# Interleaving two arrays on one core: the second x tile comes in as four DMAs with 8 KiB rows

## The chip, the cores and the metric

The kernel runs on one core of one Trainium2 chip. The metric is the device time of one execution in microseconds (us). Before the change the median of three runs is 314.51 us (314.41 to 314.53).

## The reference

Two float32 arrays x and y of shape 32 x 256 x 1024 are woven into one of shape 32 x 256 x 2048: x goes to the even places of the last axis and y to the odd ones.

```python
def reference(x, y):
    batch, seq, dim = x.shape
    result = np.zeros((batch, seq, dim * 2), dtype=np.float32)
    result[..., 0::2] = x
    result[..., 1::2] = y
    return result
```

No arithmetic is done. 33.55 MB of x, 33.55 MB of y and 67.11 MB of output are moved.

## The kernel before, in words

Since the last axis of the output is just twice as long, the arrays are taken as flat. They are cut into n = 8 tiles. A tile of x or y is 128 partitions by W = 8192 floats, so each partition holds one contiguous row of 32 KiB and the tile 4 MiB. The 8 MiB of output that belong to a tile are made in two halves h = 0, 1, each from H = 4096 columns of the x tile and of the y tile, and each stored as a tile of 128 x 8192.

There are two buffers each for x (`xt`), y (`yt`) and the output (`ot`). Tile k uses `xt[k % 2]` and `yt[k % 2]`; half h uses `ot[h]`. The program is written out by hand for three engines, which meet only through semaphores:

- SP issues all loads (queue q1 of the profile). The first x tile comes as two DMAs of half the columns (L37 and L38, rows of 16 KiB), then y 0, x 1, y 1 without any wait (L48 and L45). From tile 2 on, x (L45) waits until DVE has read the second half of the x tile two before, that is until `woven` has reached 4(k-2)+3, and y (L48) until it has reached 4(k-2)+4.
- DVE (VectorE) weaves. For each tile and half it copies the x half into the even places of `ot[h]` (L60) and the y half into the odd places (L63). Each copy counts `woven` up by one. Before L60 it waits for the x tile (`xsem`; `hsem` for the second half of the first tile) and for the store that last read `ot[h]` (`osem`); before the L63 of a first half it waits for the y tile (`ysem`).
- ACT (ScalarE) only issues stores (L68, queue q10): one of 4 MiB for each half, 16 in all, each when `woven` says that both copies of the half are done.

The loads of SP and the stores of ACT run on the same 16 DMA engines. A DMA counts its semaphore up by 16, one for each engine, as its parts land. At the end ACT waits for the last store of `ot[0]` and clears the range of semaphores, and SP waits for the last store of `ot[1]`. The wrapper moves SP's first two DMAs ahead of the opening barrier of the program.

Of the kernel before, what the change touches and what calls it, by code (L numbers as in the profile page):

```python
# [3 lines left out]


def _interleave(nc, x, y, out):
    P = 128
    W = 8192
    H = W // 2  # L10

    total = 1
    for s in x.shape:
        total *= s
    n = total // (P * W)
    assert n * P * W == total

    def rows(ap, names, k):
        flat = ap.rearrange("b s d -> (b s d)")
        return flat[k * names : (k + 1) * names].rearrange("(p w) -> p w", p=P)  # L20

    fp32 = mybir.dt.float32
    xt = [nc.alloc_sbuf_tensor(f"xt{b}", [P, W], fp32).ap() for b in (0, 1)]
    yt = [nc.alloc_sbuf_tensor(f"yt{b}", [P, W], fp32).ap() for b in (0, 1)]
    ot = [nc.alloc_sbuf_tensor(f"ot{b}", [P, W], fp32).ap() for b in (0, 1)]

    xsem = [nc.alloc_semaphore(f"xsem{b}") for b in (0, 1)]
    hsem = nc.alloc_semaphore("hsem")
    ysem = [nc.alloc_semaphore(f"ysem{b}") for b in (0, 1)]
    woven = nc.alloc_semaphore("woven")  # L30
    osem = [nc.alloc_semaphore(f"osem{b}") for b in (0, 1)]

    xs = [rows(x, P * W, k) for k in range(n)]
    ys = [rows(y, P * W, k) for k in range(n)]
    os_ = [rows(out, 2 * P * W, k) for k in range(n)]

    nc.sync.dma_start(out=xt[0][:, :H], in_=xs[0][:, :H]).then_inc(xsem[0], 16)  # L37
    nc.sync.dma_start(out=xt[0][:, H:], in_=xs[0][:, H:]).then_inc(hsem, 16)  # L38

    for k in range(n):  # L40
        b = k % 2
        if k >= 2:
            nc.sync.wait_ge(woven, 4 * (k - 2) + 3)
        if k:
            nc.sync.dma_start(out=xt[b], in_=xs[k]).then_inc(xsem[b], 16)  # L45
        if k >= 2:
            nc.sync.wait_ge(woven, 4 * (k - 2) + 4)
        nc.sync.dma_start(out=yt[b], in_=ys[k]).then_inc(ysem[b], 16)  # L48

    for k in range(n):  # L50
        b = k % 2
        for h in (0, 1):
            c = slice(h * H, (h + 1) * H)
            if h == 0:
                nc.vector.wait_ge(xsem[b], 16 * (k // 2 + 1))
            elif k == 0:
                nc.vector.wait_ge(hsem, 16)
            if k:
                nc.vector.wait_ge(osem[h], 16 * k)
            nc.vector.tensor_copy(out=ot[h][:, 0::2], in_=xt[b][:, c]).then_inc(woven, 1)  # L60
            if h == 0:
                nc.vector.wait_ge(ysem[b], 16 * (k // 2 + 1))
            nc.vector.tensor_copy(out=ot[h][:, 1::2], in_=yt[b][:, c]).then_inc(woven, 1)  # L63

    for k in range(n):
        for h in (0, 1):
            nc.scalar.wait_ge(woven, 4 * k + 2 * h + 2)
            nc.scalar.dma_start(  # L68
                out=os_[k][:, h * W : (h + 1) * W], in_=ot[h]
            ).then_inc(osem[h], 16)  # L70

    nc.scalar.wait_ge(osem[0], 16 * n)
    used = sorted(s.num for s in [*xsem, hsem, *ysem, woven, osem[0]])
    assert used == list(range(used[0], used[-1] + 1)), used
    nc.scalar.sem_clear(range(used[0], used[-1] + 1))
    nc.sync.nop(nofuse=True).wait_op(osem[1], 16 * n, "sem-ge").then_inc(
        osem[1], -16 * n
    )


def kernel(tc, x, y, out):
    nc = tc.nc
    tc.close()
    tc.compile()

    _interleave(nc, x, y, out)

    blocks = nc.main_func.blocks
    for engine in (mybir.EngineType.SP, mybir.EngineType.SP):
        opening = blocks[0].instructions  # L90
        at, moved = next(
            (b, i)
            for b in blocks[1:]
            for i in b.instructions
            if i.engine == engine and i.opcode == "DMACopy"
        )
        assert not (moved.sync_info and moved.sync_info.on_wait)
        body = at.instructions
        body.remove(moved)
        gate = next(  # L100
            n
            for n, i in enumerate(opening)
            if i.engine == engine and i.opcode == "Drain"
        )
        opening.insert(gate, moved)
        at.instructions = body
        blocks[0].instructions = opening


# [1 line left out]
_INS = ['x', 'y']  # L111
_OUTS = [((32, 256, 2048), 'float32')]


# [23 lines left out]
```

## Time and profile before

| | |
|---|---|
| median of 3 runs | 314.51 us (314.41 to 314.53) |
| the profiled execution: its time, its span | 314.29 us, 313.0 us |
| DMA queue q1 (loads): packets, share of 16 engines | 2448, 50.1% |
| DMA queue q10 (stores): packets, share of 16 engines | 2304, 49.7% |
| mean rate over the span, read and written together | 429 GB/s |
| DVE busy | 72.6 us (23%), 32 copies of 2.3 us |
| L60 idle before, waiting for stores | 171.5 us of 178.8 |
| L63 idle before, waiting for y | 46.7 us |

The span is the time between the first and the last recorded event of the profiled execution; the device time is a little more. The page gives the busy time of each engine, the DMA activity in 40 equal slices, the DMA queues, and the chain of work that ended last, followed back from the end. The timeline and the chain list start and length in microseconds from the span's start, and in brackets the idle time before an instruction with what ended it. An idle time of DVE costs nothing by itself, if the DMA engines are busy meanwhile.

### The profile page before, as it was taken

To read this page: it belongs to the slowest core of one execution; us is meant where nothing else is said; L and a number is where in the kernel's file an instruction comes from. 1 tells how busy PE (TensorE), PEld (TensorE's weight loads), DVE (VectorE), ACT (ScalarE), POOL (GpSimd) and SP (SyncE) were. 2 spreads that over 40 slices of the span, in tenths; PEclk is the share of its full clock that TensorE was granted. 3 is DMA by queue.
4 is the path that set the end of the run, shared out by engine and by line. 5 is a ranking of instruction groups with operands and counts; after the bars stand their busy time and mean duration, and the time that the engine had idled before them with its cause. 6 is when DMAs were issued, how large, how long until landed. Compare 5 with 4: busy or idle time off the path is not lost.

```text
span 313.0 us, 113 instructions
## 1 busy us (share of the span) xinstructions
DVE 72.6 (23%) x32; POOL 0.2 (0%) x4
## 2 busy tenths in 40 slices
DVE  0226002231022410325003150031501305013510
POOL 0000000000000000000000000000000000000000
DMA  8999999999999999999999999999999999999998
GB/s 341 463 410 394 469 402 448 423 436 436 419 452 406 465 402 469 402 469 402 469 402 448 423 436 436 419 452 406 465 402 469 402 469 402 465 406 444 427 431 373
DMA packets 4752, 134.22 MB, mean 429 GB/s; under 512 B 528, under 2 KB 528, under 8 KB 528
## 3 DMA queue, kind: packets, MB, share of 16 engines
q1 hardware_dynamic: 2448, 67.11, 50.1%
q10 hardware_dynamic: 2304, 67.11, 49.7%
HBM read 67.11 MB, written 67.11 MB: 429 GB/s over the span
## 4 chain that ended last, share of the span: by engine, by line
DMA 82%; DVE 12%; issue 0%
DMA out_dram<-ot 76%; DVE ot L63 6%; DMA yt<-in_y_dram 6%; DVE ot L60 6%
## 5 line engine op out<-in xcount | busy, mean ns | idle before, releaser
L60 DVE COPY ot<-xt 128x4096 f32<-128x4096 f32 x16 | 36.7, 2295 | 178.8 <-DMA out_dram<-ot 171.5
L63 DVE COPY ot<-yt 128x4096 f32<-128x4096 f32 x16 | 36.7, 2292 | 46.7 <-DMA yt<-in_y_dram 46.7
L122 POOL MEMSET const-bfloat16-1.0<- 128x1 bf16 x1 | 0.1, 101 | 0.0
L122 POOL MEMSET const-uint8-127<- 128x1 uint8 x1 | 0.1, 101 | 0.0
L122 POOL MEMSET const-float32-0.0<- 128x1 f32 x1 | 0.1, 98 | 0.2 <-issue 0.2
L122 POOL MEMSET const-float32-1.0<- 128x1 f32 x1 | 0.1, 98 | 0.0
## 6 DMA issues: line engine op xcount, KB each, us to landing
out_dram<-ot ACTq DMA_DIRECT2D x16, 4096.0 KB, 29.1
yt<-in_y_dram SPq DMA_DIRECT2D x8, 4096.0 KB, 60.8
xt<-in_x_dram SPq DMA_DIRECT2D x7, 4096.0 KB, 43.7
xt<-in_x_dram SPq DMA_DIRECT2D x2, 2048.0 KB, 9.5
```

Of the source, the lines that this page charges most:

```text
L60: nc.vector.tensor_copy(out=ot[h][:, 0::2], in_=xt[b][:, c]).then_inc(woven, 1)
L63: nc.vector.tensor_copy(out=ot[h][:, 1::2], in_=yt[b][:, c]).then_inc(woven, 1)
L122: nc = _bacc.Bacc("TRN2", target_bir_lowering=False, num_devices=1)
```

## The change

The load of the second x tile (k = 1) is cut into four DMAs of a quarter of the columns each. A row of such a DMA is 2048 floats, 8 KiB. The four are issued one after the other at the place of the one before, between y 0 and y 1. The first three count a new semaphore `qsem` (48 when all have landed), the fourth counts `xsem[1]` as the whole load did. DVE waits for `qsem` as well before the first L60 of tile 1, and the new semaphore is cleared with the others at the end. All other loads and all stores are as before, and the order of the instructions on DVE and ACT is the same.

```diff
+    qsem = nc.alloc_semaphore("qsem")
...
+    quarters = [slice(q * W // 4, (q + 1) * W // 4) for q in range(4)]
...
-        if k:
+        if k == 1:
+            for c in quarters[:3]:
+                nc.sync.dma_start(out=xt[b][:, c], in_=xs[k][:, c]).then_inc(qsem, 16)
+            c = quarters[3]
+            nc.sync.dma_start(out=xt[b][:, c], in_=xs[k][:, c]).then_inc(xsem[b], 16)
+        elif k:
             nc.sync.dma_start(out=xt[b], in_=xs[k]).then_inc(xsem[b], 16)
...
                 nc.vector.wait_ge(xsem[b], 16 * (k // 2 + 1))
+                if k == 1:
+                    nc.vector.wait_ge(qsem, 48)
...
-    used = sorted(s.num for s in [*xsem, hsem, *ysem, woven, osem[0]])
+    used = sorted(s.num for s in [*xsem, hsem, qsem, *ysem, woven, osem[0]])
```

## The prediction

> **What bounds the kernel now.** I read the page first, then the chain that ended last, then the timeline of the first tiles, then five-microsecond windows around the place of the change, and last the trace's records of single DMA packets and landings, which no view prints and which I give as numbers.
>
> The page, its head, the strip of DMA busy tenths and the queues:
>
> ```profile
> span 313.0 us, 113 instructions
> ...
> DMA  8999999999999999999999999999999999999998
> ...
> DMA packets 4752, 134.22 MB, mean 429 GB/s; under 512 B 528, under 2 KB 528, under 8 KB 528
> ...
> q1 hardware_dynamic: 2448, 67.11, 50.1%
> q10 hardware_dynamic: 2304, 67.11, 49.7%
> ```
>
> The two queues (q1 carries SP's loads, q10 ACT's stores) fill 50.1 + 49.7 = 99.8% of what 16 engines can give in the span. DVE is busy 23%. The kernel is a DMA stream without holes; only holes in it, or dearer packets, can move the time. The 528 small packets are semaphore writes (33 DMAs x 16 engines). The other 4224 are whole rows: 31 whole DMAs and 2 halves at 128 rows each make 33 x 128 = 4224. So one packet is one row, 32 KiB long, or 16 KiB in the first x tile, and each of the 16 engines takes 8 rows of every DMA.
>
> The chain (start, length, what) says what sets the order inside the stream:
>
> ```profile
> 1.90 19.98 DMA yt<-in_y_dram
> ...
> 21.90 2.30 DVE ot L63
> 24.20 2.20 DVE ot L60
> 26.40 2.21 DVE ot L63
> ...
> 28.63 38.64 DMA out_dram<-ot
> ```
>
> After that a store of 34 us and two DVE copies repeat to the end. A store takes 34 us although its 4 MiB alone would take 9.7, because two stores and the loads share the engines. The timeline shows the first tiles:
>
> ```profile
> 21.90 2.30 DVE L63 COPY ot<-yt 128x4096 f32<-128x4096 f32 x1 [12.30 <-DMA yt<-in_y_dram]
> ...
> 24.23 72.37 ACTq L68 DMA_DIRECT2D out_dram<-ot  x5
> ...
> 26.43 0.33 SPq L45 DMA_DIRECT2D xt<-in_x_dram  x1
> ...
> 48.01 2.30 DVE L60 COPY ot<-xt 128x4096 f32<-128x4096 f32 x1 [19.41 <-DMA out_dram<-ot]
> 55.22 2.29 DVE L63 COPY ot<-yt 128x4096 f32<-128x4096 f32 x1 [4.91 <-DMA yt<-in_y_dram]
> 67.29 2.30 DVE L60 COPY ot<-xt 128x4096 f32<-128x4096 f32 x1 [9.78 <-DMA out_dram<-ot]
> ```
>
> The first y tile lands at 21.9, the first store is issued at 24.23, and the second x tile runs on q1 from about 21.5, so most of it shares the engines with the first stores. In the packet records a 32 KiB row takes 1.213 us on one engine whatever the mix, a 16 KiB row 0.611, and once both queues have work they take strict turns, one row each. The windows (stretch, DVE and POOL busy, clock, DMA share by packet starts, GB/s) show the one hole after the start:
>
> ```profile
> 20.00:25.00 5.00, 3.10 (x2) 0.00 (x0) 1.00 1.11 478
> 25.00:30.00 5.00, 3.60 (x2) 0.00 (x0) 1.00 0.91 328
> 30.00:35.00 5.00, 0.00 (x0) 0.00 (x0) 1.00 0.97 419
> ```
>
> In 25 to 30 the rate falls to 328 GB/s. The packet records say why: the two load rows ahead of the first store row take 1.2 to 1.6 and 1.7 to 1.9 us instead of 1.213. Added up this is 0.74 us on each engine. It comes as the store queue starts from empty beside running loads (store issued 24.23, first store row 29.06, six rows of x done by then). No later stretch has it: from 40 to 290 us all rows together exceed 1.213 by under 0.01 us per engine. The other start of an empty queue, SP's at 1.0 us, stretched its first rows by 0.65 us.
>
> **The change, part by part.** *Issues.* SP issues four DMAs instead of one behind the first y: three more at 0.33 to 0.44 us (the rows of its issues), 1.0 to 1.3 us. Queued behind is the second y's issue, at 2.76, now near 4. Its first row cannot run before the second x is through, after 35 us, so this costs nothing; the cover is over 30 us. *The wait on qsem.* It goes into the set that DVE's L60 for the second tile waits for already; three quarters have landed before the fourth on the same queue, apart from fractions of a microsecond. Behind it on DVE stands L63, which waits for y until later. Zero.
>
> *Dearer rows.* The trace has no 8 KiB row of a load. By the landings, two 2 MiB halves take 2 x 4.88 = 9.76 us (7.28 to 12.16 is the second), a whole 4 MiB 9.67 (the last store, 303.27 to 312.94) or 9.72 (first y, 12.16 to 21.88). One cut costs 0.04 to 0.09, three cuts 0.12 to 0.27. I take 0.2 us, the three additional semaphore packets of 9 ns included. This is on the path, since the stream has no slack.
>
> *Turns.* If a turn stays one row, the second x gives 0.3 us away per turn and receives 1.2 us of store. By the time of the first store row (26 to 29 us) 15 to 23 of its 32 rows per engine are through. The first store then needs 8 x (1.21 + 0.31) = 12 us and lands near 39 to 42 instead of 47.9. The second ends at about 26.8 + 16 x 1.21 + 17 x 0.31 = 51.5 when the join is early, and near 58.5 when it is late (x exhausted after some ten turns, six store rows shared with y rows). Both lie before the second y, which ends when everything so far is through: 21.9 + four times 9.67 + 0.2 + 0.74 = 61.5 us. DVE can't make a new store without that y, so **the store queue runs empty**, which it never did between 29 and the end. The loads fill the gap (third x and y were issued at 26.4 and 28.6), so no bandwidth is lost by that alone.
>
> But from here the state is the one of 21.9 us again, a tile later: y lands, no store is queued, x and y of the next tile stand on SP's queue, and DVE goes L63, L60, L63. The store queue starts from empty a second time, at about 63.9 (61.5 + 2.35). Bounds of that start: 0 (no later stretch pays it) to 0.74, or a little more. I take 0.74, because this is the same transition with the same row sizes, and SP's start at 1.0 us paid a similar 0.65. What the first start costs with short rows beside it is not shown; between -0.74 and +0.74, I take no change, as the stretching began 1.8 us after the store's issue and so seems to follow it rather than the loads' rows.
>
> *Afterwards.* As the second tile's start repeats the first tile's, the distance between loads and stores repeats too: before, y lands at 55.2 and the second store of the tile before at 67.3, and at the end 287.5 against 293.6; this holds five store rows, enough to hide the last L63 and the next store's way to the engines (issue at 289.89, first row 293.25). Cost zero if the distance is the same.
>
> Sum: 0.20 + 0.74 = **+0.94 us**. The profiled execution has span 313.0 and time 314.29; it becomes 313.9 and 315.23. The median before is 0.22 above that execution, so the forecast is 314.51 + 0.94 = **315.45**.
>
> **The rivals.** (1) *The restart is free*, not slower: the stretch at 26 us belonged to the first store of the program, not to the queue being empty. For it: all of 40 to 290 us is clean. Against: the queue was never empty there. It decides if the second start costs under 0.43 us (0.63 less the 0.20). Time 314.51 + 0.20 = 314.7. If the first start also shrinks with short rows, 0.74 is given back: 313.97.
>
> (2) *The queue does not run empty*, the change doesn't do what it says: turns go by bytes, or by several short rows. Then landings stay as before and only 0.20 is left: 314.7. For: no mix of unequal rows is in the trace, since the 16 KiB rows ran alone. Against: with 32 KiB rows a turn was exactly one. The Trainium skill, "DMA: Bandwidth & Descriptors", section "Queues, rings and completion order", has engines change queues at packets, which hold some 9 to 17 descriptors as a rule. The one-row turns of this trace disagree for long rows; for 8 KiB rows no run here shows it yet.
>
> (3) *The distance comes back a row shorter*, five x rows ahead of the store instead of six. Then the last load leaves the queue with 1.21 us less store work, 3.36 - 1.21 = 2.15 us from issue to need at the end. A store's way to the engines lies between 1.0 us (SP's first issue to first row) and 4.83 (24.23 to 29.06), so the hole is 0 to 2.7 us; with 1 us of it the time is 316.45.
>
> (4) *Each quarter pays a gap of its own*, some 0.6 us as at SP's start: 4 x 0.65 = 2.6, time 317.1. Against: the second half of the first x followed the first at 4.88 us per 2 MiB without a gap. The Trainium skill, same page, section "Bandwidth", gives 6.15 us for 1 MB and 78% of peak there; four of these would be 24.6 us against 9.7, far more than this. The back-to-back halves of this trace speak against it.
>
> **How the numbers follow.** 0.2% of 314.5 is 0.63 us, about what a measurement of this kernel can tell from no change; so slower is over 315.14, faster under 313.88. Forecast 0.51, of which 0.47 slower and 0.04 within the bound (first start cheaper). Rival 1 0.20: 0.17 within, 0.03 faster. Rival 2 0.13, within. Rival 3 0.12 and rival 4 0.04, slower. Together slower 0.63, same 0.34, faster 0.03. The range holds rivals 1 and 2 with the lower cut cost (314.6, and 0.2 for a partly cheaper first start) and reaches to rival 3's middle: 314.4 to 316.5; left out are rival 4, half of rival 3 and the faster corner, about 0.13. The forecast's own range is 314.9 to 315.8.
>
> **What would show it.** In the changed profile: L63 of the second tile starting near 61.5 instead of 55.2, and the L60 after it with no wait on a store (before 9.78 us); the second start of stores as a window near 65 to 70 with a rate as low as the 328 here; then the old period of 38.7 us, each landing 0.9 us late. Landings that stay at 48.0 and 55.2 mean rival 2; 419 GB/s throughout 60 to 75 means rival 1; a hole before the last two stores means rival 3; quarters with gaps before the stores begin mean rival 4. The prediction is wrong if the time lies below 314.4, which needs a start that costs less than before, as nothing else in this full stream can be saved.

## The result, and the profile after

The changed kernel takes 315.03 us (median of 12 runs, 314.80 to 315.71) against 314.46 us before (12 runs, 314.26 to 314.54): +0.57 us, a ratio of 1.0019 with a 95% interval of 1.0011 to 1.0027. That is slower by a hair less than the 0.2% that the prediction called measurable from no change, and inside its range. The profiled execution has span 313.5 us and time 314.80, against 313.0 and 314.29.

The page after, head, DMA strip and queues:

```profile
span 313.5 us, 116 instructions
...
DMA  8999999999999999999999999999999999999998
...
DMA packets 5184, 134.22 MB, mean 428 GB/s; under 512 B 576, under 2 KB 576, under 8 KB 576
...
q1 hardware_dynamic: 2880, 67.11, 50.2%
q10 hardware_dynamic: 2304, 67.11, 49.6%
```

There are 432 more packets on q1: 384 short rows in excess (512 of 8 KiB for 128 of 32 KiB) and 48 semaphore writes. The stream is as full as before. The timeline of the first tiles after (L71 and L74 are the copies that were L60 and L63):

```profile
22.04 2.30 DVE L74 COPY ot<-yt 128x4096 f32<-128x4096 f32 x1 [12.30 <-DMA yt<-in_y_dram]
...
24.37 87.02 ACTq L79 DMA_DIRECT2D out_dram<-ot  x6
...
46.74 2.29 DVE L71 COPY ot<-xt 128x4096 f32<-128x4096 f32 x1 [18.00 <-DMA xt<-in_x_dram]
61.69 2.29 DVE L74 COPY ot<-yt 128x4096 f32<-128x4096 f32 x1 [12.66 <-DMA yt<-in_y_dram]
63.90 2.29 DVE L71 COPY ot<-xt 128x4096 f32<-128x4096 f32 x1
66.10 2.29 DVE L74 COPY ot<-yt 128x4096 f32<-128x4096 f32 x1
```

The order of events is the forecast one. The first store lands at 41.9 by the landing records (47.9 before), the second at 60.4 (67.3), the second y at 61.67 (55.2). The L71 at 63.90 waits for no store, where before the same copy waited 9.78 us. So the store queue runs empty and starts again at about 64 us. The windows around both starts (stretch, DVE and POOL busy, clock, DMA share, GB/s):

```profile
20.00:25.00 5.00, 2.96 (x2) 0.00 (x0) 1.00 0.98 415
25.00:30.00 5.00, 3.74 (x2) 0.00 (x0) 1.00 1.08 393
30.00:35.00 5.00, 0.00 (x0) 0.00 (x0) 1.00 1.01 436
60.00:65.00 5.00, 3.31 (x2) 0.00 (x0) 1.00 1.05 452
65.00:70.00 5.00, 3.39 (x2) 0.00 (x0) 1.00 0.99 419
70.00:75.00 5.00, 0.00 (x0) 0.00 (x0) 1.00 0.97 419
```

Here is the surprise: the second start, in 65 to 70, has the 419 GB/s of an undisturbed stretch and not the 328 of the first start before. At the end the distance between the landing of the last y (288.05) and of the store ahead (294.11) is 6.06 us, as before (287.54 and 293.60). The lines before, and then after:

```profile
287.57 2.30 DVE L63 COPY ot<-yt 128x4096 f32<-128x4096 f32 x1 [4.92 <-DMA yt<-in_y_dram]
293.62 2.29 DVE L60 COPY ot<-xt 128x4096 f32<-128x4096 f32 x1 [3.76 <-DMA out_dram<-ot]
```

```profile
288.07 2.29 DVE L74 COPY ot<-yt 128x4096 f32<-128x4096 f32 x1 [4.92 <-DMA yt<-in_y_dram]
290.40 8.60 ACTq L79 DMA_DIRECT2D out_dram<-ot  x2
294.13 2.30 DVE L71 COPY ot<-xt 128x4096 f32<-128x4096 f32 x1 [3.77 <-DMA out_dram<-ot]
```

Windows are coarse for tenths of a microsecond, so from here on I use the packet records. They can be sorted into the 16 engines, since on each engine one packet starts where the last ends. Take for each size the undisturbed spacing of rows (32 KiB 1.2095 us, 16 KiB 0.6075, 8 KiB 0.306, a semaphore write 0.005) and call **lost time** what a stretch of an engine's time holds beyond the sum of its rows. In microseconds, mean of the 16 engines:

| | before | before, again | after | after, again |
|---|---|---|---|---|
| first packet | 1.18 | 1.25 | 1.29 | 1.30 |
| lost 0 to 8 us | 0.65 | 0.66 | 0.66 | 0.61 |
| lost 24 to 34 (first store start) | 0.76 | 0.66 | 0.85 | 0.98 |
| lost 60 to 75 (second store start) | 0.00 | 0.00 | 0.09 | 0.00 |
| last packet's end, mean engine | 312.44 | 312.43 | 312.87 | 312.88 |
| last packet's end, slowest engine | 312.59 | 312.61 | 313.11 | 313.17 |

The short rows' own price is 8 x (4 x 0.306 - 1.2095) + 3 x 0.005 = 0.13 us. Mean of after less mean of before: rows 0.13, first start 0.20, second start 0.05, the first eight microseconds together 0.06; the sum, 0.44, is the 0.44 by which the mean engine ends later. The slowest engine is 0.1 further from the mean in the two profiles after, which makes 0.54, and the two profiled executions are 0.5 above the two before (314.80 and 314.86 against 314.29 and 314.30).

The order of the packets on one engine of the changed kernel from 28 us on (q a short load row, L a 32 KiB one, S a store row, a dot or comma the semaphore write of a load or store) shows the turns one by one:

```
qSqSqS.SqSqSqSqSq,qSqSqS.SLSLSL
```

### The profile page after: what moved, and what is told of

Read it like the earlier page. It is cut to its first block, busy times and chain, and to the rows that moved or that the text cites. A ratio compares the mean times of both kernels' runs of the same rounds, so it can differ in the third digit from the quotient of the medians.

```text
span 313.5 us, 116 instructions
## 1 busy us (share of the span) xinstructions
DVE 72.5 (23%) x32; POOL 0.2 (0%) x4
## 4 chain that ended last, share of the span: by engine, by line
DMA 78%; DVE 11%; another core or an unknown queue 4%; SPq 1%; issue 0%
DMA out_dram<-ot 65%; DMA xt<-in_x_dram 14%; DVE ot L71 6%; DVE ot L74 6%; SPq L50 0%; SPq L57 0%
## 5 line engine op out<-in xcount | busy, mean ns | idle before, releaser
L71 DVE COPY ot<-xt 128x4096 f32<-128x4096 f32 x16 | 36.7, 2295 | 171.7 <-DMA out_dram<-ot 146.2
L74 DVE COPY ot<-yt 128x4096 f32<-128x4096 f32 x16 | 36.7, 2292 | 54.5 <-DMA yt<-in_y_dram 54.5
```

## The experiments

Theories: A, the forecast's, each start of an empty store queue costs about 0.74 us. B, the stretch belongs to the first store of the program. C, what the change costs is the first start beside short rows. Later D, E and F on what makes that first start dear. Differences are medians against runs of the kernel before on the same chip; the ratios in brackets are 95% intervals and follow the means of the runs, so a few high runs move them more than they move the median.

**The short rows alone.**

```diff
-        nc.sync.dma_start(out=yt[b], in_=ys[k]).then_inc(ysem[b], 16)
+        if k == 0:
+            for q in range(4):
+                c = slice(q * W // 4, (q + 1) * W // 4)
+                nc.sync.dma_start(out=yt[b][:, c], in_=ys[k][:, c]).then_inc(
+                    qsem if q < 3 else ysem[b], 16)
+        else: ...
```

> Rows alone: the first y tile, which runs before any store, comes in as four DMAs with 8 KiB rows; the second x tile is whole. Nothing shares the engines with the short rows, so no turn changes, and one store-queue start stays. Both theories say: the short rows' own price, 0.15 to 0.2 us (24 additional packets and 3 semaphore packets per engine), y landing at about 22.05. If instead the rows make up the whole measured +0.57, this kernel is 0.5 to 0.6 us slower than before.

+0.01 us (314.49 against 314.48; ratio 0.9993 to 1.0011). The rows are in the profile, with 8 KiB rows spaced by 0.306 us and y landing at 22.19; the first store start lost 0.56, less than in the profiles of before, and hid them there. The rows are not the whole 0.57, and the interval, up to 0.35 us, leaves room for their 0.13.

**Four DMAs with long rows.** The same four DMAs, but cut by partitions:

```diff
+        if k == 1:
+            for q in range(4):
+                c = slice(q * P // 4, (q + 1) * P // 4)
+                nc.sync.dma_start(out=xt[b][c], in_=xs[k][c]).then_inc(
+                    qsem if q < 3 else xsem[b], 16)
```

> The second x tile as four DMAs again, but each of 32 partitions with rows of 32 KiB: the number of DMAs without the short rows. Every theory in which a turn is one row says the landings of before (first store 48, second y 55.2, second store 67.3), no empty store queue, and +0.03 to +0.05 us from three semaphore packets and their turns. If it is the number of DMAs that costs (a gap per DMA), it is +0.4 or more.

+8.79 us (323.27; ratio 1.0268 to 1.0300), which no theory had. The windows of this kernel:

```profile
20.00:25.00 5.00, 2.74 (x2) 0.00 (x0) 1.00 1.11 288
25.00:30.00 5.00, 3.96 (x2) 0.00 (x0) 1.00 1.03 210
30.00:35.00 5.00, 0.00 (x0) 0.00 (x0) 1.00 0.98 315
```

The engines are busy (share near 1) at half the rate: while these loads run alone, a 32 KiB row takes 2.55 us (median of 48) in place of 1.213. So this is no control for the number of DMAs; it shows that these loads over 32 partitions, alone on the engines, moved at half speed. The number of DMAs is settled by the quarters of the first y instead, which had no gaps between them.

**Two halves.** The quarters of the change, but two pieces of 16 KiB rows.

> The second x tile as two DMAs with 16 KiB rows. By the turn per row the store queue gets two thirds of the bytes instead of four fifths; when the second y lands, one to three rows of the second store are left, less than the 2.3 us of L63 and the way to the engines, so the queue runs empty only briefly, and the next store starts beside running loads. Theory A (each start of an empty store queue costs about 0.74): +0.8. Theory B (the stretch belongs to the program's first store; a later start is nearly free): +0.1 to +0.2, with all 32 KiB rows after 60 us at 1.213.

+0.53 us (315.01; ratio 1.0009 to 1.0027). Turns by row show again: the first store lands at 45.8 us, between 41.9 and 47.9. The second y lands at 59.3 and the second store at 65.1, and the store behind it was issued at 61.6; by the packet records no store row runs from 63.7 to 65.7, so the queue runs empty hardly at all. From 60 to 75 us 0.00 is lost, but with so little of a restart this says little against theory A. B's sum is too low, because two other terms came: the first start lost 1.03 us, and the end opened a hole:

```profile
290.44 2.30 DVE L72 COPY ot<-yt 128x4096 f32<-128x4096 f32 x1 [9.75 <-DMA yt<-in_y_dram]
292.77 6.19 ACTq L77 DMA_DIRECT2D out_dram<-ot  x2
294.09 2.29 DVE L69 COPY ot<-xt 128x4096 f32<-128x4096 f32 x1 [1.36 <-DMA out_dram<-ot]
```

(Here L72 is the copy of y and L69 that of x; the store of the copy at 290.44 is issued at 292.77.) The store ahead lands at 294.07, only three rows after the last y. Its last rows end between 293.2 and 293.7 us, engine by engine, and the first rows of the new store start at 293.61, 0.84 us after its issue. So the engines that were done early stand idle: 0.19 us on the mean as plain gaps near 293.5, and 0.13 more in slightly longer packets behind it. This is rival 3's hole, in a kernel where the distance did shrink.

**Quarters on a later tile.** `k == 3` in place of `k == 1` in the change:

> The fourth x tile (k = 3) comes in as quarters, the second whole. The program's first store start is as before (0.74 of stretch near 26 us). From about 95 us the stores overtake the loads and the store queue is empty near 125 to 143 us, for longer than in the changed kernel; then it starts once more. Theory A: rows 0.17 plus a full second start 0.74, +0.9. Theory B: rows 0.17 plus a restart of 0 to 0.1, +0.2 to +0.3. If the first start's change with short rows beside it is what costs (theory C), this kernel is at +0.2, as that start is untouched here.

+0.10 us (314.58; ratio 1.0001 to 1.0027). The windows of its program's first store start, and of the restart:

```profile
25.00:30.00 5.00, 3.53 (x2) 0.00 (x0) 1.00 0.93 341
...
135.00:140.00 5.00, 1.14 (x1) 0.00 (x0) 1.00 0.97 419
140.00:145.00 5.00, 5.00 (x3) 0.00 (x0) 1.00 0.97 419
145.00:150.00 5.00, 0.56 (x1) 0.00 (x0) 1.00 0.97 419
```

The stores end at 125.8 by the landings and the next one is issued at 141.2, so the queue stands empty for 15 us. All time lost from 110 to 280 us is 0.01 us. The restart is free, the first start lost 0.74 as whole loads do, and the mean engine ends 0.16 later than before, the rows' 0.13 and little else. The times alone say less: two of the eleven runs (315.84 and 316.55) lift the mean to 0.4 us above before, and the interval reaches to 0.85 us, just under theory A's 0.9. By the profile theory A has fallen; B and C stand.

**A small store ahead of the first.** In both kernels:

```diff
+    nc.scalar.wait_ge(xsem[0], 16)
+    nc.scalar.dma_start(out=os_[0][:, :128], in_=xt[0][:, :128]).then_inc(wsem, 16)
+    nc.scalar.wait_ge(wsem, 16)
```

(SP waits for `wsem` too before it loads the third x tile into the same buffer.)

> The kernel before, with one small store ahead of the first: ACT stores 512 B per partition (64 KiB, from the first x tile, to a place that the first whole store writes over later) when the first half of x 0 has landed, near 7.5 us. It has no short rows of x 1. Theory B (the stretch of 0.74 us belongs to the first store of the program, whatever its size): the stretch goes from 26 us to near 8 us or gets smaller, and the window 25 to 30 us is full; the time is between -0.7 and +0.1. Theory D (it belongs to a large store that begins beside running loads while the queue is empty): the stretch at 26 us stays at 0.7 and the time is +0.0 to +0.1.

+0.18 us (314.62; ratio 0.9997 to 1.0015). Lost from 24 to 34 us: 0.67. A store of 64 KiB does not take the first start away; theory B in its first form has fallen.

> The changed kernel with the same small early store. If the +0.57 of the change comes from the first store start beside short rows (theory C) and the small store takes that start away, this kernel is within 0.2 of the kernel with the small store and whole loads. If it comes from the rows or from the second start near 66 us, it stays 0.5 to 0.6 above that kernel.

+0.80 us (315.24, of 7 runs; ratio 1.0017 to 1.0039), 0.62 above its partner. As the first start was still there (0.78 lost, and 0.19 at the second), this said nothing against C. Its profile was taken of the slowest of its runs, 315.69.

**ACT's queue used early, by a load.**

```diff
-    nc.sync.dma_start(out=xt[0][:, H:], in_=xs[0][:, H:]).then_inc(hsem, 16)
+    nc.scalar.dma_start(out=xt[0][:, H:], in_=xs[0][:, H:]).then_inc(hsem, 16)
...
-    for engine in (mybir.EngineType.SP, mybir.EngineType.SP):
+    for engine in (mybir.EngineType.SP, mybir.EngineType.Activation):
```

> The kernel before with the second half of the first x tile loaded by ACT's queue in place of SP's, from the same early place in the program. Both queues start together at 1.0 us. If the stretch at 26 us is a matter of a queue's first use, a load through it is enough and it disappears: -0.5 to -0.7. If it is the first store (writes to HBM) that counts, it stays at 0.74 and the time is within 0.1 of before, apart from what the two starts at 1.0 us do to each other.

+0.13 us (314.57; ratio 0.9997 to 1.0014), and 0.58 us lost at the first store start. The queue's first use is not it.

**The changed kernel again**, unaltered:

> The changed kernel once more, unaltered, on the chip of the three kernels beside it. +0.57 as before; in its profile the first store start shows 0.8 us of stretch and small gaps beside the short rows, and the second start near 66 us at most 0.1 on the mean of the engines, with a few engines at 0.4 to 0.5.

+0.53 us (314.97; ratio 1.0008 to 1.0025). Its columns stand in the table: 0.98 at the first start, 0.00 at the second. The few engines with 0.4 to 0.5 at the second start, seen in the first profile, did not come back.

**Sixteen pieces**, 2 KiB rows:

> The second x tile as sixteen DMAs with 2 KiB rows. By the periods of 32, 16 and 8 KiB rows (1.2095, 0.6075, 0.306 us) each additional row costs an engine about 0.005 us: 15 x 8 x 0.005 = 0.6 us, and 15 semaphore packets 0.07. If the price of the changed kernel is mainly the number of rows, this kernel is at +0.7 to +0.8 with the first store start at 0.7 to 1.0. If it is mainly the first start beside short rows and that start gets worse the shorter the rows are, the stretch between 24 and 34 us is well over 1.0 and the time +1.0 to +1.5. By the forecast's full second start it would be 1.4 or more, with that stretch near 66 us.

+0.82 us (315.27; ratio 1.0018 to 1.0040). The 2 KiB rows are spaced by 0.080 us, so the rows cost 8 x (16 x 0.0803 - 1.2095) + 15 x 0.005 = 0.68 us; the first start lost 0.78, the second 0.01. So the rows' price follows the estimate and makes up most of the difference. The first start beside 2 KiB rows lost less than beside 16 KiB ones (1.03): it does not get worse the shorter the rows are.

**The kernel before again**, unaltered:

> The kernel before once more, for a second profile of its only store start beside whole rows: 0.6 to 0.75 us of stretch near 26 us, none later; time within 0.1 of before.

0.12 us above the common median, ratio 0.9990 to 1.0009; 0.66 lost at the first start and 0.00 later.

**A large store ahead of the first**, 16 KiB per partition (`:H` for `:128` in the edit above), in both kernels:

> The kernel before with a large early store: 16 KiB per partition (2 MiB, the first half of the first x tile, written over later by the first whole store), issued when that half has landed, near 7.5 us, beside running loads. 2 MiB more cost 4.86 us by themselves: 319.3. Theory E (the stretch is paid once, at the first start of a large store in the program): a stretch of 0.6 to 0.75 near 10 us and none at the store start near 31 us; 319.3. Theory F (something else at the first tile's start): the stretch stays at the store start near 31 us; 319.3 when none appears near 10 us, 320 when both do.

+5.11 us (319.60 of 5 runs; ratio 1.0150 to 1.0178), of which 4.86 are the additional 2 MiB. SP again waits for `wsem` before the third x tile. The windows of the early store and of the first output store (issued at 30.22):

```profile
10.00:15.00 5.00, 0.00 (x0) 0.00 (x0) 1.00 0.95 360
...
30.00:35.00 5.00, 4.53 (x3) 0.00 (x0) 1.00 0.97 419
35.00:40.00 5.00, 0.00 (x0) 0.00 (x0) 1.00 0.97 419
```

0.91 us are lost between 8 and 20 us, beside the 16 KiB load rows of the first x tile's second half, and 0.00 from 24 to 75. The stretch moved to the first large store and did not come again when the queue started from empty near 31 us: theory E.

> The changed kernel with the same large early store. If Theory E holds, the first start beside short rows is free here, and this kernel is above the one with whole loads by the rows alone, 0.13 us (0 to 0.25), although its store queue runs empty a second time. If the short rows make any store start dearer, it is 0.4 to 0.6 above it, with stretch near 31 us.

+5.37 us (319.86 of 4 runs; ratio 1.0158 to 1.0186), 0.26 above its partner where the change alone costs 0.57; the two sets of runs overlap (319.38 to 319.83 and 319.65 to 320.20). That is a hair above the 0 to 0.25 expected, and with so few runs the times alone don't tell 0.26 from 0.57; the profile decides. In it, 0.97 us are lost between 8 and 20, 0.00 at the store start beside the 8 KiB rows, 0.00 at the start after the queue ran empty. The mean engine ends 0.18 after its partner's: rows 0.13, the rest within what profiles differ by. With the once-paid stretch out of the way, short rows cost no more than themselves at a store start.

## Why the prediction was right, and which terms of its sum were not

**The bound and the turns: right.** One row per turn, the first store between 39 and 42 (41.9), the second y at 61.5 (61.67), no wait on a store in the L60 behind it, the distance of 6.06 us kept at the end. The second store landed at 60.4, just past the forecast's 51.5 to 58.5. Rival 2 is out: 8 KiB rows took turns one by one beside 32 KiB rows. The Trainium skill, "DMA: Bandwidth & Descriptors", section "Queues, rings and completion order", has engines switch after whole packets of typically some 9 to 17 descriptors; this trace disagrees with it for these rows. Rival 4 is out as well: the quarters of the first y and the first two of the second x landed 2.49 us apart, near the 2.42 of a quarter of a whole 4 MiB store. The Trainium skill, same page, section "Bandwidth", gives 6.15 us for 1 MB, but measured it on DMAs that GpSimd issues; for SP's, queued one behind the other, the 2.49 us of these runs decides.

**The second start: the step that failed.** "I take 0.74, because this is the same transition with the same row sizes." It is 0.05 on the mean of two profiles, 0.01 in the fourth tile's variant, and 0.00 in the pair with a large early store. The transition is the same; what differs is that a large store has run before, as the pair with a large early store shows. Rival 1 had this mechanism, with a chance of 0.20, and its time of 314.7 leaves out the next term.

**The first start: "I take no change"** was mis-sized by about +0.2. Six profiles with whole rows beside the program's first large store (before twice, first y in quarters, fourth x in quarters, small early store, ACT's early load) lost 0.56 to 0.76 us there; five with shorter rows (after twice, small early store, halves, sixteenths) lost 0.78 to 1.03, and the two large early stores, beside 16 KiB rows, 0.91 and 0.97. Between the two groups lie only 0.02 us, so the sign is better known than the size. The bound of the prediction held it, its value did not.

**The rows: 0.20** were 0.13. **The profiled execution's difference** has another 0.1 from the spread of the engines and 0.06 from the first eight microseconds, which the sum did not have; the quarters of the first y show a spread as wide (0.30 from mean to slowest) at no measurable cost, so I don't tie it to the change. That part of the 0.57 us stays open.

So +0.94 was forecast and +0.57 measured, the right sign with most of the sum under the wrong heading: 0.74 at the second start, where 0.05 was, and 0 at the first, where 0.2 was. The likeliest case's own range, 314.9 to 315.8, holds the result for a reason it did not give: that one term too large and others too small nearly met is luck.

Open: what the once-paid stretch is. It needs more than a 64 KiB store and more than a use of the queue, and it is paid by the first large store, whether at 8 or 26 us. What the engines do in it no record here tells. No version tried is faster than the kernel before; the stretch can be moved, and was not removed.

## What to carry to other kernels

When a DMA stream has no holes, changing the row size of one load changes who waits for whom (one row per turn, so the queue with longer rows overtakes) but, here, hardly the end: count the added rows at their undisturbed spacing, and check that the distance between the last load and the store ahead of it survives, as three rows left a hole of 0.3 us where five left none. A cost seen once in a trace, at the first time that something happens, is not a price per occurrence: before it is multiplied, look for a second occurrence, or make one.

## What the runs showed of the hardware

- The first large store of the program, beside running loads, stretched the packets by 0.56 to 1.03 us per engine; later starts from an empty store queue cost 0.00 to 0.19.
- Alone on the engines, a load of 32 partitions took 2.55 us per 32 KiB row against 1.213 for 128 partitions, although all 16 engines were busy; cutting one 4 MiB load that way cost 8.79 us.
- SP stood still in issuing when many DMAs were queued. In the kernel with sixteen pieces:

```profile
2.28 21.45 SPq L48 DMA_DIRECT2D xt<-in_x_dram  x16
...
23.78 0.53 SPq L55 DMA_DIRECT2D yt<-in_y_dram  x1
...
28.69 3.63 SPq L55 DMA_DIRECT2D yt<-in_y_dram  x1
```

The sixteen issues end at 23.7 us, by which time the first pieces were landing (22.6); three of them, between 5.3 and 19.3 us, take 2.79, 7.24 and 3.89 us, the others 0.4 to 1.2. The four quarters were issued within 2 us. What held SP is not shown. It cost nothing here, because the loads ahead kept the engines busy.
